# Attention values a unit later, and the split of moved blocks behind q's parts

## The chip, the cores and the metric

The kernel runs on one core of a Trainium2 chip. The time is device time in microseconds (us) for one execution. A core has five engines that work beside each other and wait for one another by semaphores: TensorE (PE in the profile; its weight loads are the row PEld), VectorE (DVE), ScalarE (ACT), GpSimd (POOL) and SyncE (SP), whose queue here issues most DMAs. Each engine takes its instructions in the order in which the program wrote them.

## The reference

One encoder block on 256 tokens of width 2048, in float32:

```
h = RMSNorm(x); [q | k | v | u] = h @ w_in
a = windowed attention: 12 query heads, 4 key/value heads of 128, |t-s| <= 128,
    ALiBi bias, a sink logit per head, softmax
f = Fourier mix of u in 4 groups of 128 channels
x = x + concat(RMSNorm(a), RMSNorm(f)) @ w_out
x = x + down(GELU(conv3(h2 @ w_gate)) * (h2 @ w_value)),  h2 = RMSNorm(x)
y = RMSNorm(x)
```

## The kernel before

Every matrix product is made with operands split in a high and a low part (`fp32r`), three products for one. So every weight tile is loaded by SP as `raw` (1 MB), copied to its high part by ScalarE (L185) and subtracted to its low part by VectorE (L186); these make `parts`. TensorE consumes one weight tile in one *unit*. The units go: 0 to 3 u, 4 to 7 v, 8 to 23 the heads of keys and queries, 24 to 39 the output projection `w_out`, then the feed-forward part.

Units 8 to 23 hold k0 q0 q1 q2, k1 q3 q4 q5, k2 q6 q7 q8, k3 q9 q10 q11. A query head whose product is in unit s passes through these steps in later units; the number is the distance from s:

- 1: its two product halves are summed (`qk_out`: ScalarE copies one half, L637; VectorE adds, L639) and made into parts (`qk_parts`: tile `qT`, ScalarE L234, VectorE L235).
- 2: TensorE multiplies by the keys (`scores`, L665, six products); VectorE adds the bias and takes the maximum (`scores_out`, L681, L685, L686); ScalarE exponentiates (`exps`, L695).
- 3: VectorE scales by the sums (`weigh`, L704, L705, L708; tile `sc`) and transposes in blocks of 32 (`turn`, L715; tile `tb`); SP writes the blocks to DRAM (tile `turn`, L720).
- 4: SP fetches the blocks back in moved order, in four DMAs (`fetch`, L726; tile `td`).
- 5: the moved blocks are split in parts (`turn_out`; tile `pt`, ScalarE L739, VectorE L740).
- 6: TensorE multiplies by the values (`values`, L768, six products into `ps_o`); ScalarE squares the result (L492) and makes its scaled high part (L234, tile `cat`), VectorE the low part (L235); GpSimd adds the square to a running sum (L497, not for head 0).

The last head, 11, skips the way through DRAM: TensorE transposes it at distance 4 (`turn_last`, L750), and its values are at 5.

The order on each engine is the program's order. In unit i the program writes: the lists `before` (values, the last head's transposes, scores), then the unit's own products, then `beside`, then the split of the weights of unit i + 2 with the load of the weights of unit i + 5 behind it on SP (`step`, `split`), and then `behind` (the exponentials). In `beside` of a unit stand, in this order: fetch, q's sum, the split of moved blocks, the last head's split, the scaling, the block transposes with their write-out, k's sum and the parts of q or k, the scores' bias and maximum, and the feature (`values_out`). The values that TensorE uses in a unit therefore need the block split of an earlier unit, and the scores in a unit the parts of q from the unit before.

Tiles used in turn: `pt`, `td`, `qT` and the sums have two buffers, `sc` and `tb` one, the weights' `raw` and `parts` three each. The units' products and, up to unit 23, the value products rotate through four PSUM banks (`mm`); scores and the value products from unit 24 on rotate through four others (`dn`). Unit 26 is the first whose products read the features of heads 4 to 7; units 29 and 31 read those of heads 8 to 11.

Of the kernel before, what the change touches and what calls it, by code (L numbers as in the profile page):

```python
# [18 lines left out]
NH = 12  # L19
# [77 lines left out]
def block_kernel(  # L97
# [316 lines left out]
    before, beside, behind = {}, {}, {}  # L414

    def at(when, i, f, *a):
        when.setdefault(i, []).append((f, a))
# [217 lines left out]
    def qk_out(kind, h, ps):  # L635
        tmp = ph.tile([P, S], F32, tag="tmp", name=f"tmp_{kind}{h}", bufs=2)
        nc.scalar.activation(tmp, ps[:, S : 2 * S], AF.Copy)  # L637
        add = ph.tile([P, S], F32, tag="add", name=f"add_{kind}{h}", bufs=2)
        nc.vector.tensor_tensor(add, ps[:, 0:S], tmp, ALU.add)  # L639
        if kind == "k":  # L640
            nc.vector.tensor_tensor(add, add, r1b, ALU.mult)
        st["add", kind, h] = add
# [135 lines left out]
        feature_out(ps, h, vcol(V_GA + h), sq_a, h == 0)  # L778


    slot_of = {kh: N_QK + n for n, kh in enumerate(QK_ORDER)}
    for i in range(N_QK, N_OUT + 8):
        heads = {i - s: h for (kind, h), s in slot_of.items() if kind == "q"}
        new = [kh for kh, s in slot_of.items() if i - s == 1]
        if i - 9 in range(NG):
            at(before, i, fourier_channels, i - 9)
        valued = [h for d, h in heads.items() if d == (5 if h == NH - 1 else 6)]
        for h in valued:
            at(before, i, values, h, mm if i < N_OUT else dn)
        turned = {d: h for d, h in heads.items() if h < NH - 1}  # L790
        last = {d: h for d, h in heads.items() if h == NH - 1}
        if 4 in last:
            at(before, i, turn_last, last[4])
        if i == 15:
            at(before, i, total, sq_f, "f")
        if 2 in heads:
            at(before, i, scores, heads[2])
        if 4 in turned:
            at(beside, i, fetch, turned[4])

        for kind, h in new:
            if kind == "q":
                at(beside, i, lambda k=kind, h=h: qk_out(k, h, st.pop(("ps", k, h))))
        if 5 in turned:
            at(beside, i, turn_out, turned[5])
        if 4 in last:
            at(beside, i, turn_last_out, last[4])
        if 3 in heads:
            at(beside, i, weigh, heads[3])
        if 3 in turned:  # L810
            at(beside, i, turn, turned[3])
        for kind, h in new:
            if kind == "k":
                at(beside, i, lambda k=kind, h=h: qk_out(k, h, st.pop(("ps", k, h))))
            at(beside, i, qk_parts, kind, h)
        if 2 in heads:
            at(beside, i, scores_out, heads[2])
            at(behind, i, exps, heads[2])
        for h in valued:
            at(beside, i, values_out, h)  # L820
# [60 lines left out]
    for n, (c, kq) in enumerate(OUT_ORDER):  # L881
        i = N_OUT + n
# [391 lines left out]
    i = up_index[n]  # L1274
# [156 lines left out]
```

## Time and profile before

| | |
|---|---|
| Median of 3 runs | 910.96 us (910.14 to 911.5) |
| Profiled execution | 908.96 us |
| Its span, first to last instruction | 907.2 us |
| TensorE / VectorE / ScalarE / GpSimd busy | 893.2 / 753.1 / 545.9 / 54.3 us |
| Granted TensorE clock | 0.998 |
| Busy in 122 to 150 us (28.0 us): TensorE, VectorE, ScalarE, GpSimd | 26.20, 24.50, 18.43, 2.67 us |

In the trace, TensorE begins the work of unit 15 at 91.00 us, of unit 19 at 118.36, of unit 23 at 145.90 and of unit 27 at 173.52; the output projection's first product is at 156.13. VectorE's first instruction of `beside` stands at 91.14 us for unit 14, 96.24 for 15, 102.46 for 16, 110.28 for 17, 118.38 for 18, 123.50 for 19, 130.52 for 20, 137.82 for 21, 145.96 for 22, 151.07 for 23, 158.31 for 24 and 166.25 for 25. So VectorE works on a unit's list while TensorE is already in the next one.

A line of a timeline has the start in us, the duration in us, the engine, the program line, the operation, the tile written and the tiles read, their shapes and the count of merged instructions. In square brackets is the idle time of the engine before the instruction and what ended it. A line of the waits has the waiting engine, tile and line, what it waited for, the total in us, how many times, and the longest.

### The profile page before, as it was taken

The numbers are of one execution on the slowest core, as the hardware profiler recorded it, in microseconds if no ns is written. First come the engines' busy times: TensorE is split into PE (matmuls) and PEld (weight loads), VectorE is DVE, ScalarE is ACT, GpSimd is POOL, SyncE is SP. The second block draws the span as 40 slices with busy tenths as digits, with TensorE's granted clock in tenths as the row PEclk, the third lists the DMA queues.
The fourth block names the chain that finished last, engine by engine and source line by source line (L and its number), as shares of the span: only waits on it lengthen the run. The fifth ranks groups of instructions, "written<-read, shape, count | busy, mean of one in ns | idle before, by whom it ended". The sixth has DMA issues, their size and how long they took to land.

```text
span 907.2 us, 12781 instructions
## 1 busy us (share of the span) xinstructions
PE 893.2 (98%) x5020; PEld 804.0 (89%) x5020; DVE 753.1 (83%) x905; ACT 545.9 (60%) x661; POOL 54.3 (6%) x65
## 2 busy tenths in 40 slices
PE   9999999999999999999999999999999999999996
PEld 7899888888899999999999999999999999999885
DVE  7569888777678877889887998978988789998996
ACT  7757576655565656557565566566656566656544
POOL 0001010110000000000000000000000000000004
PEclk9999999999999999999999999999999999999999
DMA  9965666655559687677988779797888987779652
GB/s 360 340 233 174 211 231 197 229 189 191 203 228 290 219 260 235 197 264 215 295 238 276 243 271 278 256 295 232 279 243 244 308 272 255 243 245 286 213 197 92
DMA packets 40827, 220.62 MB, mean 243 GB/s; under 512 B 4512, under 2 KB 10528, under 8 KB 16448
## 3 DMA queue, kind: packets, MB, share of 16 engines
q1 hardware_dynamic: 36512, 190.06, 56.7%
q0 software_dynamic: 4112, 29.49, 17.3%
q8 instruction: 39, 0.64, 0.3%
q10 hardware_dynamic: 144, 0.26, 0.1%
q14 instruction: 20, 0.16, 0.0%
HBM read 214.81 MB, written 4.98 MB: 242 GB/s over the span
## 4 chain that ended last, share of the span: by engine, by line
PE 81%; DVE 8%; DMA 3%; issue 3%; ACT 3%; POOL 1%; SPq 1%; ACTq 0%; POOLq 0%; DVEq 0%
PE ps_val L395 17%; PE ps_gate L395 17%; PE ps_gate L397 8%; PE ps_val L397 8%; PE ps_P L1148 3%; PE ps_P L1150 3%; PE ps_P L1149 3%; PE ps_N L1148 2%; PE ps_N L1150 2%; PE ps_N L1149 2%; DVE parts L186 2%; PE ps_u L289 2%; DMA td<-turn 2%; PE ps_a L380 2%; PE ps_a L378 2%
## 5 line engine op out<-in xcount | busy, mean ns | idle before, releaser
L186 DVE TENSOR_TENSOR parts<-raw,parts 128x2048 fp32r<-128x2048 f32 (+1 forms) x129 | 293.1, 2272 | 43.4 <-ACT parts L185 42.7
L185 ACT ACTIVATE parts<-raw 128x2048 fp32r<-128x2048 f32 (+1 forms) x129 | 245.1, 1901 | 41.7 <-PE ps_a L380 11.9
L395 PE MATMUL ps_val<-hU,parts 128*128 128x512 f32 x688 | 227.7, 382 | 0.0
L395 PE MATMUL ps_gate<-hU,parts 128*128 128x512 f32 x688 | 227.3, 382 | 0.0
L397 PE MATMUL ps_val<-hU,parts 128*128 128x256 f32 x688 | 187.5, 273 | 0.0
L397 PE MATMUL ps_gate<-hU,parts 128*128 128x256 f32 x688 | 186.9, 273 | 0.0
L395 PEld LDWEIGHTS ps_val<-hU,parts 128*128 128x128 f32 x688 | 130.0, 189 | 18.1
L395 PEld LDWEIGHTS ps_gate<-hU,parts 128*128 128x128 f32 x688 | 130.0, 189 | 18.1
L397 PEld LDWEIGHTS ps_val<-hU,parts 128*128 128x128 f32 x688 | 132.0, 192 | 0.8
L397 PEld LDWEIGHTS ps_gate<-hU,parts 128*128 128x128 f32 x688 | 131.8, 192 | 0.9
L926 ACT ACTIVATE ft_g<-ps_gate 128x256 f32<-128x256 f32 x43 | 16.5, 384 | 112.9 <-PE ps_gate L397 110.3
L395 PE MATMUL ps_q<-hT,parts 128*128 128x512 f32 x192 | 62.2, 383 | 0.0
L926 ACT ACTIVATE ft_v<-ps_val 128x256 f32<-128x256 f32 x43 | 16.5, 383 | 73.3 <-PE ps_val L397 73.3
L1148 PE MATMUL ps_P<-parts_P,op_P 128*128 128x512 f32 x144 | 54.7, 380 | 0.0
L1149 PE MATMUL ps_P<-parts_P,op_P 128*128 128x512 f32 x144 | 54.6, 379 | 0.0
L1150 PE MATMUL ps_P<-parts_P,op_P 128*128 128x512 f32 x144 | 54.6, 379 | 0.0
L397 PE MATMUL ps_q<-hT,parts 128*128 128x256 f32 x192 | 50.4, 273 | 0.0
L1034 DVE TENSOR_TENSOR parts_N<-sumw,parts_N 128x2048 fp32r<-128x2048 f32 x18 | 41.2, 2289 | 9.9 <-ACT parts_N L1033 9.9
L1148 PE MATMUL ps_N<-parts_N,op_N 128*128 128x512 f32 x108 | 41.0, 380 | 0.0
L1149 PE MATMUL ps_N<-parts_N,op_N 128*128 128x512 f32 x108 | 40.9, 379 | 0.0
L1150 PE MATMUL ps_N<-parts_N,op_N 128*128 128x512 f32 x108 | 40.9, 379 | 0.0
L395 PEld LDWEIGHTS ps_q<-hT,parts 128*128 128x128 f32 x192 | 36.1, 189 | 4.7
(347 smaller groups left out, 1554.8 us busy)
## 6 DMA issues: line engine op xcount, KB each, us to landing
raw<-in_w_up SPq DMA_DIRECT2D x86, 1024.0 KB, 6.1
raw<-in_w_in SPq DMA_DIRECT2D x20, 1024.0 KB, 5.7
sumw<-in_w_down POOLq DMA_DIRECT2D x18, 1024.0 KB, 8.5
raw<-in_w_out SPq DMA_DIRECT2D x16, 1024.0 KB, 4.8
raw<-in_w_down_late SPq DMA_DIRECT2D x4, 1024.0 KB, 5.7
u_raw<-in_u_in SPq DMA_DIRECT2D x4, 768.0 KB, 10.5
raw<-in_w_down_last SPq DMA_DIRECT2D x4, 768.0 KB, 4.6
turn<-tb SPq DMA_DIRECT2D x11, 256.0 KB, 4.2
```

What stands on the lines that cost most here:

```text
L185: nc.scalar.activation(hi, raw, AF.Copy)
L186: nc.vector.tensor_tensor(lo, raw, f32(hi), ALU.subtract)
L289: nc.tensor.matmul(ps_u[b], block(hk(k), part, b, True), in_turn(w), start=k == 0 and n == 0, stop=k == NK - 1 and n == 2,)
L378: nc.tensor.matmul(ps, ah, wh, start=first and q == q0, stop=False)
L380: nc.tensor.matmul(ps, ah, wl, start=False, stop=last and q == q0 + len(kk) - 1)
L395: nc.tensor.matmul(ps, hi[:, s], in_turn(h), start=k == 0, stop=False)
L397: nc.tensor.matmul(ps[:, 0:S], lo[:, s], in_turn(h)[:, 0:P], start=False, stop=k == NK - 1)
L926: nc.scalar.activation(tmp, ps[:, S : 2 * S], AF.Copy)
L1034: nc.vector.tensor_tensor(lo, src, f32(hi), ALU.subtract)
L1148: nc.tensor.matmul(ps, o[:, 0, p, :], wh, start=first and p == 0, stop=False)
L1149: nc.tensor.matmul(ps, o[:, 1, p, :], wh, start=False, stop=False)
L1150: nc.tensor.matmul(ps, o[:, 0, p, :], wl, start=False, stop=end)
```

## The change

Two things are changed in the schedule of units 8 to 31. The value products of heads 0 to 8 are at distance 7 instead of 6, with the feature and the running sum that follow them in the same unit; heads 9 and 10 stay at 6 and head 11 at 5. Head 6's product so moves from unit 23 to unit 24, and from the first group of PSUM banks to the second. And in `beside`, the split of the moved blocks is written behind the parts of q or k and ahead of the scores' bias, not right behind q's sum.

```diff
+    VALUES = {NH - 3: 6, NH - 2: 6, NH - 1: 5}
     slot_of = {kh: N_QK + n for n, kh in enumerate(QK_ORDER)}
     for i in range(N_QK, N_OUT + 8):
...
-        valued = [h for d, h in heads.items() if d == (5 if h == NH - 1 else 6)]
+        valued = [h for d, h in heads.items() if d == VALUES.get(h, 7)]
...
         for kind, h in new:
             if kind == "q":
                 at(beside, i, lambda k=kind, h=h: qk_out(k, h, st.pop(("ps", k, h))))
-        if 5 in turned:
-            at(beside, i, turn_out, turned[5])
         if 4 in last:
             at(beside, i, turn_last_out, last[4])
         if 3 in heads:
             at(beside, i, weigh, heads[3])
         if 3 in turned:
             at(beside, i, turn, turned[3])
         for kind, h in new:
             if kind == "k":
                 at(beside, i, lambda k=kind, h=h: qk_out(k, h, st.pop(("ps", k, h))))
             at(beside, i, qk_parts, kind, h)
+        if 5 in turned:
+            at(beside, i, turn_out, turned[5])
         if 2 in heads:
             at(beside, i, scores_out, heads[2])
             at(behind, i, exps, heads[2])
         for h in valued:
             at(beside, i, values_out, h)
```

## The prediction

> **What bounds the kernel now.** I read the page first (busy time, the slices), then the waits of the attention stage alone, then that stage's timeline engine by engine.
>
> ```profile
> PE 893.2 (98%) x5020; PEld 804.0 (89%) x5020; DVE 753.1 (83%) x905; ACT 545.9 (60%) x661; POOL 54.3 (6%) x65
> ```
>
> TensorE carries the time, so the change can move the end only where TensorE stands still. The waits from 44 to 200 us (the waiting instruction, its releaser; us in total, times, longest) say where that is:
>
> ```profile
> ACT pt L739 <- DMA td<-turn: 17.4, 8, 3.8
> ...
> DVE pt L740 <- ACT pt L739: 8.3, 7, 2.1
> ...
> PE ps_o L768 <- DVE pt L740: 2.7, 4, 0.9
> PE ps_s L665 <- DVE qT L235: 2.3, 3, 0.9
> ```
>
> TensorE waits 5.0 us in all, for two things that VectorE makes: the split of the moved blocks (pt) and q's parts (qT). ScalarE waits 17.4 us for the blocks' DMA, and VectorE 8.3 us behind ScalarE. No VectorE wait in that view is on TensorE, so in this stage VectorE sets the pace. Its rows for units 18 to 20:
>
> ```profile
> 118.38 0.42 DVE L639 TENSOR_TENSOR add_q<-ps_q,tmp_q 128x256 f32<-128x256 f32 x1
> 118.71 0.68 DVE L740 TENSOR_TENSOR pt<-td,pt 128x512 fp32r<-128x512 f32 x1
> 119.31 0.16 DVE L704 TENSOR_TENSOR sm<-sm,ex 128x2 f32<-128x2 f32 x1
> ...
> 119.71 0.62 DVE L708 TENSOR_SCALAR sc<-sc,ex 128x256 f32<-128x256 f32 x2
> ...
> 120.99 0.38 DVE L235 SCALAR_TENSOR_TENSOR qT<-add_q,qT 128x256 fp32r<-128x256 f32 x1
> 121.30 2.28 DVE L186 TENSOR_TENSOR parts<-raw,parts 128x2048 fp32r<-128x2048 f32 x1
> 123.50 0.42 DVE L639 TENSOR_TENSOR add_q<-ps_q,tmp_q 128x256 f32<-128x256 f32 x1
> 125.47 0.69 DVE L740 TENSOR_TENSOR pt<-td,pt 128x512 fp32r<-128x512 f32 x1 [1.56 <-ACT pt L739]
> ...
> 126.47 0.40 DVE L681 CUSTOM_DVE_ANT_0 sc<-ps_s,rel 128x256 f32<-128x256 f32 x1
> ...
> 127.60 0.48 DVE L235 SCALAR_TENSOR_TENSOR cat<-ps_o,vec,cat 128x256 fp32r<-128x256 f32 x1
> 128.31 2.29 DVE L186 TENSOR_TENSOR parts<-raw,parts 128x2048 fp32r<-128x2048 f32 x1 [0.24 <-ACT parts L185]
> 130.52 0.42 DVE L639 TENSOR_TENSOR add_q<-ps_q,tmp_q 128x256 f32<-128x256 f32 x1
> ...
> 132.01 1.03 DVE L708 TENSOR_SCALAR sc<-sc,ex 128x256 f32<-128x256 f32 x2
> ...
> 137.82 0.15 DVE L704 TENSOR_TENSOR sm<-sm,ex 128x2 f32<-128x2 f32 x1
> ```
>
> VectorE spends 5.12 us on unit 18, 7.02 on unit 19 (1.56 of it waiting for blocks) and 7.30 on unit 20. TensorE's row shows the dependence: it resumes at 121.43, just after qT ends (120.99 + 0.38).
>
> ```profile
> 121.43 0.71 PE L665 MATMUL ps_s<-kT,qT 128*128 128x256 f32 x4 [0.93 <-DVE qT L235]
> ...
> 156.13 0.38 PE L378 MATMUL ps_a<-parts,cat 128*128 128x512 f32 x1
> ...
> 161.32 0.38 PE L768 MATMUL ps_o<-pt,v_hi 128*128 128x256 f32 x2
> ...
> 161.98 1.14 PE L665 MATMUL ps_s<-kT,qT 128*128 128x256 f32 x6
> 162.96 0.38 PE L378 MATMUL ps_a<-parts,cat 128*128 128x512 f32 x1
> ...
> 168.14 0.38 PE L378 MATMUL ps_a<-parts,cat 128*128 128x512 f32 x1
> ...
> 175.00 0.72 PE L750 MATMUL ps_t<-ident,sc 128*128 128x128 f32 x4
> 175.48 0.46 PE L378 MATMUL ps_a<-parts,cat 128*128 128x512 f32 x1
> ```
>
> Six value products take 0.66 us (161.32 to 161.98), an output unit's own products 5.18 (162.96 to 168.14). Unit 25 begins its products 6.83 us after unit 24, and 5.18 + 2 x 0.66 would do: 0.33 lost. Unit 27 should begin them 0.66 + 0.48 us (the transposes) after 168.14 + 5.18, at 174.46, and begins at 175.48: 1.02 lost.
>
> **The change, part by part.** It adds and removes no instruction; 9 heads' value products, feature copies and running sums move a unit on, and 11 block splits move behind q's parts. ScalarE's and SP's rows that price it:
>
> ```profile
> 118.83 0.44 ACT L234 ACTIVATE qT<-add_q 128x256 fp32r<-128x256 f32 x1 [0.56 <-DVE add_q L639]
> ...
> 124.81 0.63 ACT L739 ACTIVATE pt<-td 128x512 fp32r<-128x512 f32 x1 [3.47 <-DMA td<-turn]
> ...
> 125.73 0.37 ACT L492 ACTIVATE sq<-ps_o 128x256 f32<-128x256 f32 x1
> 126.00 0.47 ACT L234 ACTIVATE cat<-ps_o,vec 128x256 fp32r<-128x256 f32 x1
> 126.36 1.92 ACT L185 ACTIVATE parts<-raw 128x2048 fp32r<-128x2048 f32 x1
> ```
>
> *Value products a unit later.* The wait on pt goes: a block split made in VectorE's unit 18 is now read in unit 20, not 19. What is late next is qT in the same units (19 and 23), so this alone gains nothing there.
>
> *q's parts ahead of the split.* In units 14, 18, 22 qT comes earlier by the split's place, 119.31 - 118.71 = **0.60 us**, and TensorE's exit from units 15, 19, 23 with it. It is counted once, because between exits VectorE's pace decides.
>
> *ScalarE's queue in units 18 and 22.* Counted from the sum's start: q's high part begins at 0.45 (118.83 - 118.38); it and the blocks' high part take 0.92 (124.81 to 125.73), then come the moved square 0.27 and feature 0.36, and the weight split's high half 1.92: its end is 3.92. VectorE's half starts at 3.95 (the same 0.03 as 128.31 after 126.36 + 1.92) and takes 2.20: the unit lasts 6.15 instead of 5.12, **1.03 longer**. The moved feature half on VectorE (0.48) is covered by that wait. In unit 14, with no values yet, it is 3.32 + 2.20 = 5.52: 0.40 longer.
>
> *Units 19 and 23.* The sum now lets q's high part start at 0.45, the blocks' follows, 1.37; weight split 3.29; VectorE's half 3.32 to 5.52, against 7.02: **1.50 shorter**. VectorE's own row of work fits (pt from 1.5, 0.6; scores 126.47 to 127.60, 1.13). It needs the blocks landed by 6.15 + 0.85 = 7.00 after 118.38; they landed 6.43 after it. SP's fetch stands behind the weight load of unit 17 as before, so that does not move; the slack is 0.57. Units 18 and 19 together: **0.47 shorter**. Unit 15 waits less, so units 14 and 15 together gain about 0.1.
>
> ```profile
> 97.41 0.69 DVE L740 TENSOR_TENSOR pt<-td,pt 128x512 fp32r<-128x512 f32 x1 [0.75 <-ACT pt L739]
> ...
> 103.40 0.69 DVE L740 TENSOR_TENSOR pt<-td,pt 128x512 fp32r<-128x512 f32 x1 [0.52 <-ACT pt L739]
> ...
> 104.39 0.88 DVE L708 TENSOR_SCALAR sc<-sc,ex 128x256 f32<-128x256 f32 x2
> ...
> 159.38 0.69 DVE L740 TENSOR_TENSOR pt<-td,pt 128x512 fp32r<-128x512 f32 x1 [0.66 <-ACT pt L739]
> ```
>
> *Units 16, 20, 24.* The blocks now have three instructions more before VectorE wants them, so the waits 0.52 (unit 16) and 0.66 (unit 24) go. Unit 16's scaling falls from 0.88 to 0.62, since its value head is now head 0, which has no running sum on GpSimd: **0.78 shorter**.
>
> *GpSimd's running sum.* It moves with the values, and it holds VectorE up:
>
> ```profile
> 131.89 0.74 POOL L497 TENSOR_TENSOR sq_a<-sq_a,sq 128x256 f32<-128x256 f32 x1 [4.78 <-ACT sq L492]
> ...
> 165.59 1.33 POOL L497 TENSOR_TENSOR sq_a<-sq_a,sq 128x256 f32<-128x256 f32 x1 [4.73 <-ACT sq L492]
> ```
> ```profile
> 166.25 0.69 DVE L704 TENSOR_TENSOR sm<-sm,ex 128x2 f32<-128x2 f32 x1
> ```
>
> The two-column sum that takes 0.15 at 137.82 took 0.69 at 166.25 and ended with GpSimd's add, at 166.9. In units 18, 20, 22 the square would end at 0.45 + 0.92 + 0.37 = 1.74 and an add of 0.74 at 2.5; qT's low half is due at 120.99 - 118.38 - 0.60 = 2.01. Bounds: nothing, if VectorE is there first, and 0.54 (0.69 - 0.15). I take **0.49**, as the add would have begun first. In unit 20 it stands against the scaling's 1.03 becoming 0.62: nothing. In units 18 and 22 VectorE's delay is covered by the split's wait, but TensorE's exit loses 0.49.
>
> The Trainium skill, page "SBUF — State Buffer", section "SBUF: two separate sides", calls this pair of ports an exclusive lock: a VectorE instruction with two SBUF inputs waits for the whole GpSimd instruction, and the other way round. The rows' scaling (1.03 against 0.62) would allow a partial delay of 0.41 and a time 0.1 us shorter; the two-column row speaks for the rule.
>
> *Sum.* VectorE at unit 22: 0.1 + 0.78 + 0.47 + 0 = 1.35 earlier. TensorE's exit from unit 23: 1.35 + 0.60 - 0.49 = 1.46. Behind it head 6's value products are now still to do, +0.66. With another 0.47 and 0.66, VectorE is 2.5 us ahead at unit 25, so the losses 0.33 and 1.02 go. Gain: 1.46 - 0.66 + 0.33 + 1.02 = **2.15 us**. Head 7's feature, wanted by unit 26's seventh to twelfth products, moves with VectorE too and stays in time. From there TensorE runs without a gap, so the gain reaches the end. The profiled execution took 908.96, 2.0 under the median of 910.96; on the median the forecast is 908.8.
>
> **Rivals.** (a) *GpSimd's add comes second and qT first.* The add's start is only 0.25 us ahead of qT. Then units 20 and 22 each give 0.49 back: gain 3.1, 907.8. (b) *TensorE waits for nothing*: all 5.0 us go, 906.0. Against it: VectorE's round stays longer than TensorE's. (c) *ScalarE's new wait eats what the DMA wait gave*: units 19 and 23 shrink by 1.03 only, unit 16 alone stays; with small parts of the last losses the gain is about 0.7, 910.3. For it: ScalarE's chain leaves nothing to spare in units 18 and 22. (d) *Slower: the blocks land later.* The write-out is issued 0.6 us earlier, now amid the fetch of the head before. If the blocks land 2.1 us later than in the rows, units 15, 19, 23 keep their length less the feature: then +0.40, +0.55 and +0.08 (units 14, 18, 20) less 0.26 (unit 16), less 0.11 for qT, +0.66 for head 6, and +0.63 more at unit 27 from units 22 to 24: 2.0 slower, 913.0. It begins past the 0.57 slack and decides from about 2.1. Against it, the view of the blocks' tile:
>
> ```profile
> DMA to landing us min/median/max: 3.6/4.7/5.4
> ```
>
> **How the numbers follow.** Chances: forecast 0.41, (a) 0.22, (b) 0.06, (c) 0.16, (d) 0.15. No change means within 0.2% (1.8 us), about what a measurement of this kernel can tell. The forecast is near that bound: 0.32 of its 0.41 is taken as faster, 0.09 as within. Faster 0.32 + 0.28 = 0.60, same 0.25, slower 0.15. The range reaches from (b), 905.9, to half of (d), 912.0.
>
> **What would show it.** Right: no TensorE wait on pt; its waits on qT stay in units 19 and 23, about 1.5 us each; VectorE's wait on ScalarE for the weight split (L186) grows by some 0.6 in units 18 and 22; ScalarE's wait for the blocks' DMA falls below 6 us; unit 27 loses nothing. Wrong: TensorE waiting for cat in unit 26, or for qT over 2.3 us; the blocks landing past 7.0 after unit 18's sum; qT 0.4 instead of 0.9 long or not delayed would be (a).

## The result and the profile after

The changed kernel takes 906.18 us, median of 5 runs (905.88 to 906.72), against 910.7 (909.1 to 911.5) for the kernel before on the same chip: a ratio of 0.9953 with a 95% interval of 0.9939 to 0.9968, so 4.3 us less (2.9 to 5.6). The profiled execution took 905.88, which is 3.08 under the 908.96 of the profiled execution before.

The page's busy time of the changed kernel: no engine does less work than before, so the gain is time in which TensorE stood still.

```profile
PE 893.2 (99%) x5020; PEld 806.3 (89%) x5020; DVE 753.7 (83%) x905; ACT 546.4 (60%) x661; POOL 56.8 (6%) x65
```

The waits of the changed kernel from 44 to 200 us (engine, tile and line, releaser; us in total, times, longest):

```profile
ACT qT L234 <- DVE add_q L639: 17.6, 12, 2.4
...
DVE parts L186 <- ACT parts L185: 8.3, 8, 1.3
...
ACT pt L739 <- DMA td<-turn: 5.5, 4, 3.2
...
DVE pt L740 <- ACT pt L739: 1.8, 2, 1.5
PE ps_s L665 <- DVE qT L235: 1.7, 2, 1.0
```

TensorE's wait on pt (2.7 before) is not in the list any more. Its wait on qT is 1.7 us for VectorE's half, with 0.5 more for ScalarE's half (2.3 in all before). ScalarE waits 5.5 us instead of 17.4 for the blocks' DMA, and VectorE 1.8 instead of 8.3 for ScalarE's part of the split. ScalarE's idle time now stands ahead of q's high part (17.6 us, for q's sum), where no block holds it.

The timeline of the changed kernel for units 18 to 20, VectorE's rows, and in unit 18 ScalarE's and GpSimd's with them:

```profile
117.13 0.42 DVE L639 TENSOR_TENSOR add_q<-ps_q,tmp_q 128x256 f32<-128x256 f32 x1
...
118.01 0.61 ACT L739 ACTIVATE pt<-td 128x512 fp32r<-128x512 f32 x1
...
118.53 0.37 ACT L492 ACTIVATE sq<-ps_o 128x256 f32<-128x256 f32 x1
118.79 0.47 ACT L234 ACTIVATE cat<-ps_o,vec 128x256 fp32r<-128x256 f32 x1
118.97 0.73 POOL L497 TENSOR_TENSOR sq_a<-sq_a,sq 128x256 f32<-128x256 f32 x1 [5.17 <-ACT sq L492]
119.14 0.90 DVE L235 SCALAR_TENSOR_TENSOR qT<-add_q,qT 128x256 fp32r<-128x256 f32 x1
119.14 1.93 ACT L185 ACTIVATE parts<-raw 128x2048 fp32r<-128x2048 f32 x1
119.95 0.68 DVE L740 TENSOR_TENSOR pt<-td,pt 128x512 fp32r<-128x512 f32 x1
...
120.55 0.48 DVE L235 SCALAR_TENSOR_TENSOR cat<-ps_o,vec,cat 128x256 fp32r<-128x256 f32 x1
...
121.11 2.29 DVE L186 TENSOR_TENSOR parts<-raw,parts 128x2048 fp32r<-128x2048 f32 x1
...
123.31 0.42 DVE L639 TENSOR_TENSOR add_q<-ps_q,tmp_q 128x256 f32<-128x256 f32 x1
...
124.32 0.48 DVE L235 SCALAR_TENSOR_TENSOR qT<-add_q,qT 128x256 fp32r<-128x256 f32 x1 [0.58 <-ACT qT L234]
...
124.83 0.69 DVE L740 TENSOR_TENSOR pt<-td,pt 128x512 fp32r<-128x512 f32 x1
...
126.64 2.29 DVE L186 TENSOR_TENSOR parts<-raw,parts 128x2048 fp32r<-128x2048 f32 x1
...
128.84 0.42 DVE L639 TENSOR_TENSOR add_q<-ps_q,tmp_q 128x256 f32<-128x256 f32 x1
...
135.54 0.15 DVE L704 TENSOR_TENSOR sm<-sm,ex 128x2 f32<-128x2 f32 x1
```

Unit 18 lasts 123.31 - 117.13 = 6.18 us, unit 19 128.84 - 123.31 = 5.53, unit 20 135.54 - 128.84 = 6.70; before they took 5.12, 7.02 and 7.30. The weight split in unit 18 starts 0.04 us after ScalarE's half ends (119.14 + 1.93 = 121.07): in that unit ScalarE's queue, longer by the moved square and feature, sets VectorE's pace. VectorE's own list ends almost level with it, at 120.55 + 0.48 = 121.03, because q's low half took 0.90; the run without the running sum, below, separates the two. In unit 19 the blocks are there (124.17 on ScalarE), and the 1.56 us wait is gone.

TensorE's timeline of the changed kernel at the places that the prediction named (exit from unit 23, first product of unit 24, values and scores before unit 25, values and transposes before unit 27, first product of the feed-forward part):

```profile
146.51 0.71 PE L665 MATMUL ps_s<-kT,qT 128*128 128x256 f32 x4 [0.70 <-DVE qT L235]
...
153.64 0.38 PE L378 MATMUL ps_a<-parts,cat 128*128 128x512 f32 x1
...
158.82 0.38 PE L768 MATMUL ps_o<-pt,v_hi 128*128 128x256 f32 x2
...
160.16 0.38 PE L378 MATMUL ps_a<-parts,cat 128*128 128x512 f32 x1
...
171.19 0.39 PE L768 MATMUL ps_o<-pt,v_hi 128*128 128x256 f32 x2
...
172.22 0.46 PE L378 MATMUL ps_a<-parts,cat 128*128 128x512 f32 x1
...
179.00 0.38 PE L378 MATMUL ps_ff<-parts,cat 128*128 128x512 f32 x1
```

Unit 24 begins 156.13 - 153.64 = 2.49 us earlier than before. The stretch before unit 25 is 160.16 - 158.82 = 1.34, which is six value products and six scores at 0.66 each and nothing lost; the one before unit 27 is 172.22 - 171.19 = 1.03, no more than products and transposes need. The feed-forward part begins 3.08 us earlier than before, where its first product stood at 182.08, and 3.08 is the whole difference of the two profiled executions.

### The profile page after: what moved, and what is told of

Read it like the earlier page. It is cut to its first block, busy times and chain, and to the rows that moved or that the text cites. A ratio compares the mean times of both kernels' runs of the same rounds, so it can differ in the third digit from the quotient of the medians.

```text
span 904.1 us, 12781 instructions
## 1 busy us (share of the span) xinstructions
PE 893.2 (99%) x5020; PEld 806.3 (89%) x5020; DVE 753.7 (83%) x905; ACT 546.4 (60%) x661; POOL 56.8 (6%) x65
## 4 chain that ended last, share of the span: by engine, by line
PE 90%; DVE 4%; issue 2%; ACT 2%; POOL 1%; ACTq 0%; POOLq 0%; DVEq 0%
PE ps_val L395 17%; PE ps_gate L395 17%; PE ps_val L397 8%; PE ps_gate L397 8%; PE ps_P L1150 3%; PE ps_P L1151 3%; PE ps_P L1152 3%; PE ps_q L395 3%; PE ps_N L1150 2%; PE ps_N L1152 2%; PE ps_N L1151 2%; PE ps_u L289 2%; PE ps_a L378 2%; PE ps_a L379 2%; PE ps_a L380 2%
## 5 line engine op out<-in xcount | busy, mean ns | idle before, releaser
L185 ACT ACTIVATE parts<-raw 128x2048 fp32r<-128x2048 f32 (+1 forms) x129 | 245.2, 1902 | 41.7 <-PE ps_a L380 12.1
```

The lines of the kernel that those rows point to most:

```text
L185: nc.scalar.activation(hi, raw, AF.Copy)
```

## The experiments

Each kernel was run in five rounds beside the kernel before (4 to 12 runs of each); where no other base is named, the edit is made on the changed kernel. The intervals are those of the ratio to the kernel before. Kernels that ran on one chip can also be compared with one another: the values alone, the split alone, the loads and the second run of the changed kernel on one; the square, the parts, the fetch and the features on another; the last four on a third.

**The changed kernel again**, beside the next three.

> The changed kernel once more, beside the kernel before on one chip. In its first profile the clock granted to TensorE was 0.53 to 0.62 from 94 to 98 us. VectorE's pace: without that dip the waits of TensorE on qT in unit 19 return (about 1.2 us instead of 0.17) and the time is the same, since VectorE's instants do not move. Rival (the dip cost 1.66 us of the time): a profile without it is 1.5 us shorter, near 902.5.

906.44 us (905.42 to 906.58), ratio 0.9952 [0.9940, 0.9965]. This run also settles a doubt about the first profile, in which the granted TensorE clock fell for some 4 us inside unit 15. That stretch in the first profile (busy us, with instructions, of TensorE, its weight loads, VectorE, ScalarE and GpSimd; then the clock, 0.57, the DMA share and GB/s):

```profile
94.00:98.00 4.00, 4.00 (x16) 3.52 (x17) 3.25 (x4) 1.57 (x4) 0.00 (x0) 0.57 0.70 213
```

TensorE's scores in units 19 and 23 of the second profile, whose clock was steady:

```profile
120.02 0.71 PE L665 MATMUL ps_s<-kT,qT 128*128 128x256 f32 x4 [0.95 <-DVE qT L235]
...
146.95 0.71 PE L665 MATMUL ps_s<-kT,qT 128*128 128x256 f32 x4 [1.39 <-DVE qT L235]
```

With the dip TensorE was late, and then hardly waited in unit 19; at full clock it came early and waited 0.95. VectorE began unit 20 at 128.84 in both, and the profiled executions took 905.88 and 906.50. TensorE had slack there, so VectorE sets the time; the dip cost nothing that can be seen.

Such a dip is not peculiar to that execution. Six of the fourteen profiles of this case have one or two in this stage: the changed kernel's first, the values alone, the split alone, the loads, the square and the fetch. In the split alone the clock is 0.63 from 96 to 100 us, in the loads 0.57 from 148 to 152. In slices of half a microsecond the granted clock is 0.50, half of full speed, for about 3.5 us (7 in one case). Each dip starts during, or less than a microsecond after, a wait of TensorE of 0.9 to 3.6 us. Such a wait does not always bring one: the second profile here has a wait of 1.02 us at the same place, ended at 93.83, and no dip. The three kernels with k's sum first, at the end of this section, have none in their profiles.

**The values a unit later, the split left at its old place.**

```diff
+        if 5 in turned:
+            at(beside, i, turn_out, turned[5])
         if 4 in last:
             at(beside, i, turn_last_out, last[4])
...
-        if 5 in turned:
-            at(beside, i, turn_out, turned[5])
```

> The value products a unit later, the block split left in its old place. VectorE's pace (my theory): TensorE's waits on pt go in units 19 and 23, but its exits stay bound by q's parts, which end where they ended (2.99 us after the sum), so nothing is gained there; the moved square and feature lengthen units 18 and 22 by about 0.4 and shorten 19 and 23 by as much, and head 6's products stand behind the exit (+0.66). Some of the loss at unit 27 goes. Together 0.5 slower to 0.7 faster than before; TensorE's waits on qT grow to about 5 us in sum, ScalarE's wait for the blocks' DMA stays above 13. Rival (what counts is that the values are not ready): the 2.7 us of waits on pt are saved, 2.5 faster or more.

910.13 us, ratio 0.9999 [0.9991, 1.0008]: nothing. The waits, 44 to 200 us:

```profile
ACT pt L739 <- DMA td<-turn: 16.8, 8, 3.5
...
PE ps_s L665 <- DVE qT L235: 4.2, 3, 2.1
```

TensorE's wait on pt is gone and its wait on VectorE's half of qT has grown from 2.3 to 4.2 (0.6 more is for ScalarE's half). The blocks' DMA holds ScalarE as long as before.

**The split moved, the values left where they were.**

```diff
-        valued = [h for d, h in heads.items() if d == VALUES.get(h, 7)]
+        valued = [h for d, h in heads.items() if d == VALUES.get(h, 6)]
```

> The block split behind q's parts, the value products at the old distance of 6. VectorE's pace: the rounds of VectorE shorten as in the whole change (ScalarE's wait for the blocks falls below 7 us), but the values of units 15, 19 and 23 now wait for a split that ends 0.6 later than q's parts: TensorE waits about 3 us on pt in each, none on qT. Gain at unit 23's exit about 1.5 of VectorE less 0.6: 0.5 to 1.5 us faster than before, a quarter of the whole. Rival 1 (order alone carries it): 4 us faster. Rival 2 (a later split can only delay the values): 2 slower.

910.25 us, ratio 0.9997 [0.9987, 1.0008]: nothing either in the median, where 0.5 to 1.5 faster was expected. The waits:

```profile
ACT pt L739 <- DMA td<-turn: 4.5, 2, 2.9
...
PE ps_o L768 <- DVE pt L740: 2.7, 3, 1.2
...
PE ps_o L768 <- ACT pt L739: 1.7, 2, 1.4
```

Now the wait on qT is gone, and TensorE waits for pt 4.4 us: the value products want the split in the very next unit, and the split comes late in VectorE's list. So each half by itself trades one TensorE wait for the other: TensorE's waits for the two tiles are 5.0 us before, 4.8 and 4.4 with one half, and 2.2 and 3.9 in the two profiles with both. Two halves that give nothing in the median make a whole of some 4 us.

The nothing of this run needs a reserve. Its twelve times follow the mean granted clock of the execution: six runs at 0.992 or 0.993 took 911.3 us in the mean, three at 0.997 or 0.998 took 908.3. The kernel before, on the same chip, took 911.4 at 0.993 (5 runs) and 909.9 at 0.997 or more (12 runs). So where the clock stays up, the split alone seems worth 1.6 us, close to what was expected, and where it dips nothing is left; three runs do not settle it.

**The kernel before, with SP's weight loads behind the next fetch.** The loads that SP issues with the splits of weights 14 to 30 now wait for the fetch of the following unit. This asks how much of the gain is the blocks' landing alone.

```diff
         halves[i] = hi, lo
+        if 14 <= i <= 30:
+            held_loads.append(i + RAW)
+            return
         load(i + RAW)
...
             at(beside, i, fetch, turned[4])
+        at(beside, i, lambda: [load(held_loads.pop(0)) for _ in held_loads[:]])
```

> The kernel before, but SP issues each weight load of units 13 to 29 behind the next unit's fetch of moved blocks, not ahead of it; nothing else moves. So the fetch no longer stands behind a load that waits for VectorE's weight split. VectorE's pace: in units 19 and 23 the blocks land about 1.7 us earlier, VectorE's waits behind ScalarE for pt fall from 8.3 to about 4, its rounds shorten by about 1.4 and the time falls by 2 to 3.5 us. Rival (the wait for the blocks is slack, only the order of q's parts and of the values decides): within 0.5 of before, the waits fall and TensorE's waits stay at 5.0.

907.83 us, ratio 0.9974 [0.9965, 0.9983]: 2.4 us faster than before, as expected. VectorE's splits of the blocks in units 18, 19 and 20 (L744 is L740 of the other kernels):

```profile
117.74 0.68 DVE L744 TENSOR_TENSOR pt<-td,pt 128x512 fp32r<-128x512 f32 x1
122.84 0.68 DVE L744 TENSOR_TENSOR pt<-td,pt 128x512 fp32r<-128x512 f32 x1
130.96 0.69 DVE L744 TENSOR_TENSOR pt<-td,pt 128x512 fp32r<-128x512 f32 x1 [2.37 <-ACT pt L743]
```

The wait in unit 19 (1.56 before) is gone, and unit 20 has one of 2.37 instead: the blocks of a later head land late, and VectorE's total wait for this split fell only from 8.3 to 6.4 us, where about 4 was expected. Blocks in time for units 19 and 23, less the new wait, are so worth 2.4 us without the rest of the change, a little over half of the 4.4 (0.48% of 910) that the changed kernel gave on this chip.

**The square written behind the scaled feature.** ScalarE's queue in value units was meant to give qT's low half its turn before GpSimd's add.

```diff
-        nc.scalar.activation(one.rearrange("p (a e) -> p a e", a=2), ps, AF.Square)
         t = cat_pool.tile([P, 512], F32R, tag="cat", name=f"cat{slot}")
         split_scaled(hi_lo(t), ps, g)
+        nc.scalar.activation(one.rearrange("p (a e) -> p a e", a=2), ps, AF.Square)
```

> The changed kernel with ScalarE's square behind its scaled copy of the feature instead of ahead of it, so GpSimd's running sum starts about 0.4 us later. Port theory (mine): in units 18 and 22 q's low part on VectorE now starts first, takes 0.38 to 0.48 instead of 0.82 to 0.90, TensorE's waits on qT there shrink by about 0.45 each, and as VectorE's own list in these units was held by the weight split only to within 0.1, its round shortens a little too: 0.3 to 0.9 us faster than the changed kernel. Rival (the long q parts are only covered work): the same within 0.2.

923.98 us, ratio 1.0148 [1.0134, 1.0162]: 13.8 us slower than before, and 17.9 slower than the kernel of the next experiment on the same chip, which is as fast as the changed one. The expectation was wrong in sign, though q's low half did shrink to 0.38 us in unit 18, as it said. ScalarE and VectorE in its unit 18 (L494 is the square):

```profile
124.28 0.48 DVE L235 SCALAR_TENSOR_TENSOR cat<-ps_o,vec,cat 128x256 fp32r<-128x256 f32 x1
124.85 0.39 ACT L494 ACTIVATE sq<-ps_o 128x256 f32<-128x256 f32 x1 [1.72 <-DVE cat L235]
125.13 1.90 ACT L185 ACTIVATE parts<-raw 128x2048 fp32r<-128x2048 f32 x1
...
127.06 2.29 DVE L186 TENSOR_TENSOR parts<-raw,parts 128x2048 fp32r<-128x2048 f32 x1 [2.31 <-ACT parts L185]
```

The square and VectorE's half of the feature read the same PSUM tile, the only tile that both touch, and the later reader in program order waits for the earlier one. So ScalarE stands still for 1.72 us until VectorE has read, its half of the weight split comes after that, and VectorE waits 2.25 to 2.31 for it in the units with values, which become 1.7 to 2.4 us longer than in the changed kernel; over the stage VectorE's wait on L185 is 27.4 us instead of 8.3. The Trainium skill, page "PSUM — Partial Sum Buffer", section "PSUM bank collisions raise a hardware error", says that accesses of different engines to one bank must be ordered, reads against reads included; the trace agrees in that the second read waited, for 1.72 us. The loss is also the strongest evidence that ScalarE's queue up to the weight split is what VectorE's round hangs on.

**q's parts ahead of the block transposes.**

```diff
             at(beside, i, weigh, heads[3])
+        for kind, h in new:
+            if kind == "q":
+                at(beside, i, qk_parts, kind, h)
         if 3 in turned:
...
-            at(beside, i, qk_parts, kind, h)
+                at(beside, i, qk_parts, kind, h)
```

> The changed kernel with q's parts on VectorE ahead of the block transposes, not behind them. Theory (q's parts in units 14, 18 and 22 release TensorE): they end about 0.6 us earlier, and in 18 and 22 before GpSimd's sum starts, so another 0.4; TensorE's waits on qT in units 15, 19 and 23 fall from about 1.0 to 1.5 to 0.1 to 0.5 each. Counted once, 0.6 to 1.1 us faster than the changed kernel, and the round of VectorE is as long as before, so no more. The write-out of the blocks is 0.35 later, which the slack of 0.5 or more in units 19 and 23 covers. Rival (VectorE's round alone decides, TensorE catches up later anyway): same within 0.2.

906.07 us, ratio 0.9953 [0.9941, 0.9965]: the same as the changed kernel, where 0.6 to 1.1 faster was expected. VectorE's parts of q come 0.9 us earlier in unit 18 (118.23 against 119.14), but the unit is no shorter (6.15 us against 6.18), because VectorE then waits 0.45 us for ScalarE's half of the weight split. Over the stage VectorE waits 9.5 us for the weight split (8.3 in the changed kernel) and 2.5 for ScalarE's split of the blocks (1.8), 0.46 of it new in unit 20. The expectation feared a later write-out of the blocks; in unit 18 SP issues it no later (119.44 against 119.59), so why unit 20 waits is not shown.

**The fetch behind the write-out on SP.**

```diff
-        if 4 in turned:
-            at(beside, i, fetch, turned[4])
...
             at(beside, i, turn, turned[3])
+        if 4 in turned:
+            at(beside, i, fetch, turned[4])
```

> The changed kernel with SP's fetch of one head's blocks behind the write-out of the next head's, so the blocks of units 15, 18, 19, 22 and 23 land about 2 to 2.8 us later; the work of every engine is the same. Theory (landing past the slack of about 0.6 is paid by VectorE, since VectorE's list stands behind the blocks' split): VectorE waits 1 to 2 us in each of units 15, 19 and 23 again, ScalarE's wait for the blocks' DMA rises from 5 to over 10; 2 to 4.5 us slower than the changed kernel, about the time of the kernel before. Rival (with the values a unit later the blocks have a whole unit of slack): within 0.5 of the changed kernel.

908.27 us, ratio 0.9976 [0.9966, 0.9986]: half of the gain is lost, at the low end of what was expected. VectorE's split of the blocks in unit 23:

```profile
153.79 0.69 DVE L740 TENSOR_TENSOR pt<-td,pt 128x512 fp32r<-128x512 f32 x1 [1.76 <-ACT pt L739]
```

Blocks that land late bring the old wait back (4.0 us in the stage instead of 1.8; ScalarE's own wait is 6.8, below the 10 expected). Only SP's order was changed, so blocks landing in time are a condition of the gain.

**The features of units 18 and 22 behind the weight split.**

```diff
-            at(beside, i, values_out, h)
+            at(behind if i in (18, 22) else beside, i, values_out, h)
```

> The changed kernel with the features of heads 2 and 5 (units 18 and 22) behind the weight split instead of ahead of it. Theory (in these units ScalarE's queue sets the weight split, 1.03 us longer than before the change): the split starts 0.63 earlier on ScalarE, VectorE's units 18 and 22 last about 5.9 instead of 6.15, and GpSimd's sum no longer meets q's parts, so TensorE's exits gain another 0.45: 0.7 to 1.2 us faster than the changed kernel. Rival (TensorE's exits do not see ScalarE's queue): units as long as before, same within 0.2.

905.59 us, ratio 0.9947 [0.9935, 0.9960]: some 0.5 us under the kernel with q's parts ahead of the transposes, on the same chip, and with intervals that overlap it is no measured gain, where 0.7 to 1.2 was expected. The mechanism is visible on VectorE:

```profile
119.16 0.38 DVE L235 SCALAR_TENSOR_TENSOR qT<-add_q,qT 128x256 fp32r<-128x256 f32 x1
120.47 2.29 DVE L186 TENSOR_TENSOR parts<-raw,parts 128x2048 fp32r<-128x2048 f32 x1 [0.33 <-ACT parts L185]
122.68 0.48 DVE L235 SCALAR_TENSOR_TENSOR cat<-ps_o,vec,cat 128x256 fp32r<-128x256 f32 x1
```

q's low half takes 0.38 instead of 0.90, and the weight split starts 120.47 - 119.16 = 1.31 after it instead of 1.97. But the feature is then paid in unit 19, which is 5.93 us long instead of 5.53. Units 18 and 19 together are 0.25 us shorter (11.46 against 11.71); most of the price is moved, not removed.

**No running sum on GpSimd.** The edit leaves out the sum of squares of heads 1 to 11.

```diff
-        if not first:
+        if not first and slot >= NH:
             nc.gpsimd.tensor_tensor(sq, sq, one, ALU.add)
```

> The changed kernel without GpSimd's running sum of the attention squares (the sum keeps head 0's square only, so the attention's norm is wrong; nothing else is left out). Port theory: q's parts of units 18, 22 and 24 on VectorE take 0.38 to 0.48 instead of 0.82 to 1.0, the two-column sum of unit 25 0.15 instead of 0.70; TensorE's waits on qT in units 19 and 23 shrink by 0.45 each. As ScalarE's weight split holds VectorE's units 18 and 22 at 6.15 anyway, only the last of these waits counts: 0.3 to 0.9 us faster than the changed kernel. Rival (their length comes from something else, as the write-out or ScalarE beside them): they stay 0.8 or longer, the time stays.

905.23 us (904.88 to 905.32), ratio 0.9941 [0.9926, 0.9957]: about 1.0 us under the changed kernel by the ratios, beside an expected 0.3 to 0.9. The two kernels ran on different chips and their intervals overlap, so the size is not settled; the mechanism is. VectorE in unit 18:

```profile
119.15 0.38 DVE L235 SCALAR_TENSOR_TENSOR qT<-add_q,qT 128x256 fp32r<-128x256 f32 x1
...
121.11 2.29 DVE L186 TENSOR_TENSOR parts<-raw,parts 128x2048 fp32r<-128x2048 f32 x1 [0.58 <-ACT parts L185]
```

The same instruction at the same moment (119.14 in the changed kernel) takes 0.38 without GpSimd's add and 0.90 with it: the add costs it 0.52. The weight split starts at 121.11 in both, so the delay of qT hides under ScalarE's queue for VectorE, as forecast, and only TensorE's exits feel it.

**k's sum at the head of the list.** The rounds with k still have a wait of VectorE on ScalarE (kT's high part). In the changed kernel, unit 17:

```profile
109.07 0.15 DVE L704 TENSOR_TENSOR sm<-sm,ex 128x2 f32<-128x2 f32 x1
...
112.50 0.82 DVE L655 TENSOR_TENSOR kT<-add_k,kT 128x256 fp32r<-128x256 f32 x1 [0.90 <-ACT kT L654]
```

```diff
         for kind, h in new:
-            if kind == "q":
-                at(beside, i, lambda k=kind, h=h: qk_out(k, h, st.pop(("ps", k, h))))
+            at(beside, i, lambda k=kind, h=h: qk_out(k, h, st.pop(("ps", k, h))))
...
         for kind, h in new:
-            if kind == "k":
-                at(beside, i, lambda k=kind, h=h: qk_out(k, h, st.pop(("ps", k, h))))
             at(beside, i, qk_parts, kind, h)
```

> The changed kernel with k's two sums on VectorE at the head of units 13, 17 and 21, as q's sum is, so ScalarE makes k's high part while VectorE scales and transposes. Theory (VectorE's round sets the pace): its wait of 0.9 for k's high part goes, units 17 and 21 last about 7.2 instead of 8.05, TensorE's exits from units 19 and 23 come 0.9 and up to 1.7 earlier, then TensorE itself begins to bound: 0.9 to 1.8 us faster than the changed kernel. The write-out of these units is 0.85 later; the fetch behind it stands behind a weight load anyway. Rival (what bounds is only the order inside units 14, 18 and 22): same within 0.3.

903.16 us (902.95 to 903.8), ratio 0.9920 [0.9905, 0.9936]: about 3.0 us under the changed kernel, more than the 0.9 to 1.8 expected. VectorE in units 17 and 18:

```profile
107.97 0.42 DVE L639 TENSOR_TENSOR add_k<-ps_k,tmp_k 128x256 f32<-128x256 f32 x1
...
110.44 0.90 DVE L655 TENSOR_TENSOR kT<-add_k,kT 128x256 fp32r<-128x256 f32 x1
...
114.99 0.42 DVE L639 TENSOR_TENSOR add_q<-ps_q,tmp_q 128x256 f32<-128x256 f32 x1
```

The wait is gone, and unit 17 is 114.99 - 107.97 = 7.02 long instead of 117.13 - 109.07 = 8.06. VectorE's waits for kT fell from four to one, so three rounds are shorter by about 1 us each. VectorE begins unit 22 at 140.95, 2.68 us earlier than in the changed kernel, and the profiled execution is 2.72 shorter (903.16 against 905.88): TensorE followed VectorE's pace one for one, which is more than the expectation had credited.

**k's sum first and the two features behind.**

```diff
+            at(beside, i, lambda k=kind, h=h: qk_out(k, h, st.pop(("ps", k, h))))
...
-            at(beside, i, values_out, h)
+            at(behind if i in (18, 22) else beside, i, values_out, h)
```

> The last edit together with the features of heads 2 and 5 behind the weight split. Theory: the gains add as long as VectorE's round is longer than TensorE's: 1.3 to 2.3 us faster than the changed kernel; TensorE's waits on qT in units 19 and 23 together under 1.5. Rival (both only take away the same wait): no better than the better one alone.

903.27 us, ratio 0.9920 [0.9904, 0.9935]: no better than k's sum alone, where 1.3 to 2.3 under the changed kernel with the two gains added was expected. The features' place adds nothing that can be measured.

**All three.** The last kernel with q's parts also ahead of the transposes; the edit is shown against that kernel.

```diff
             at(beside, i, weigh, heads[3])
+        for kind, h in new:
+            if kind == "q":
+                at(beside, i, qk_parts, kind, h)
...
-            at(beside, i, qk_parts, kind, h)
+            if kind == "k":
+                at(beside, i, qk_parts, kind, h)
```

> The last two edits and q's parts ahead of the block transposes. Theory: with VectorE's rounds shorter, q's parts 0.6 earlier now count at every exit, and TensorE's waits in units 19 and 23 are nearly gone: 1.5 to 2.8 us faster than the changed kernel. Rival: the blocks' write-out, 0.35 later on top of 0.85, makes VectorE wait for the blocks again in units 19, 20 and 23, and it is slower than without this third edit.

902.62 us (902.24 to 903.18), ratio 0.9914 [0.9898, 0.9929], the lowest median here: 7.8 us under the kernel before by the ratio, 3.5 under the changed kernel. The 0.5 us to k's sum alone lies within the intervals. Its waits of TensorE:

```profile
PE ps_o L768 <- DVE pt L740: 0.7, 2, 0.3
...
PE ps_s L665 <- DVE qT L235: 0.2, 1, 0.2
```

Of the 5.0 us that TensorE waited here before, 0.9 are left, and it is busy 155.14 of the 156.00 us from 44 to 200 (150.73 before): in this stage TensorE itself is the bound now.

## Why the prediction was right, and where its size was off

The direction and the mechanism were right; the size was not. The gain is 4.3 us where 2.15 was forecast, and 906.18 lies only 0.3 above the lower end of the range. That end was rival (b)'s time, and (b) did not come true, so that the range held is in part luck.

*The bound.* VectorE's round sets the pace and TensorE follows. It holds: a slow clock of TensorE in unit 15 cost nothing, 1.7 to 2.4 us more in VectorE's units with values cost 17.9 in all, and 1 us less in three of its rounds gave 3.0.

*Value products alone gain nothing, qT is late next.* It holds: 0.9999, with the wait moved from pt to qT. What the prediction did not say is that the other half alone gains nothing in the median too: its 0.60 for q's parts ahead of the split, and the shorter units 19 and 23, need the later values, and without them TensorE waits 4.4 us on pt.

*Lengths of units.* Forecast 6.15 for units 18 and 22 and 5.52 for 19 and 23; measured 6.18 and 5.53 in units 18 and 19, 6.13 and 5.55 in 22 and 23. For these units ScalarE's queue, counted instruction by instruction, was a good model.

*Size, first part: VectorE's gain up to unit 22 was 1.35 in the sum and came out as 2.33* (145.96 before, 143.63 after, although the stage began 0.36 us later). Three terms were too small. Units 14 and 15 together became 0.43 us shorter (5.42 + 5.47 after, 5.10 + 6.22 before) instead of 0.1; the 0.1 had no working, and the count made for unit 19, 5.52 for each of the two, would have given 0.28. Unit 16 became 1.14 shorter instead of 0.78 (7.82 to 6.68): beside the wait of 0.52 and the scaling's 0.26, the instruction behind qT's low half started 0.59 us after it before (105.95 to 106.54, the scores' bias) and starts 0.34 after it now, 0.25 less. Unit 20 became 0.60 shorter instead of 0 (7.30 to 6.70): there rival (a) came true. In the second profile it did not; the unit's split of the blocks is

```profile
131.20 1.19 DVE L740 TENSOR_TENSOR pt<-td,pt 128x512 fp32r<-128x512 f32 x1
```

1.19 instead of 0.68 long, so that GpSimd's add took back 0.5 us. There the add began at 131.02, before the split; in the first profile both are recorded at 131.20, and the split kept its 0.68. So less than 0.2 us decides which of the two is held up, and it differs from one execution to the next. In units 18 and 22 the add came first, as the sum had it: qT took 0.90 and 0.82, against a forecast of 0.87.

*The rest of the sum.* From VectorE at unit 22 the steps give 2.33 + 0.60 - 0.49 = 2.44 at TensorE's exit from unit 23; unit 24 began 2.49 earlier. The losses of 0.33 and 1.02 before units 25 and 27 went, and the 0.66 for the values that moved behind the exit was paid, ahead of unit 26: 2.49 + 0.33 + 1.02 - 0.66 = 3.18, and 3.26 was measured at unit 27 (175.48 to 172.22). Then 0.18 was lost by the feed-forward part, which leaves 3.08. No step of the sum failed in sign.

*Size, second part: the base.* 908.8 was 910.96 less 2.15, which supposed that the changed kernel's profiled execution would lie 2.0 under its median too. It lay 0.3 under it. Of the 2.6 us between forecast and result, 1.7 are this and 0.9 the terms above. Why a usual execution of the kernel before takes 1 to 2 us more than the profiled one was not shown by any trace here, and stays open; its 29 runs on one chip spread from 909.0 to 912.6, the 5 of the changed kernel there from 905.4 to 906.6. The runs show a part of it: the profiled execution had no dip and a mean granted clock of 0.998, and of those 29 runs the five at 0.993 took 911.4 us in the mean, the twelve at 0.997 or more 909.9. That dips lengthen the others is likely, since the dip in the changed kernel's first profile made TensorE 1.75 us late at unit 16 (101.37 against 99.62 in the second), and where TensorE has no slack that is time lost. But no trace of a long execution of the kernel before was kept, and even at the higher clocks the mean stays 0.9 above 908.96.

*Signs to look for.* No wait on pt: right. Waits on qT in 19 and 23 of about 1.5: 0.95 and 1.39 in the profile with a steady clock. ScalarE's wait for blocks below 6: 5.5. Unit 27 loses nothing: right. The weight split's wait on ScalarE growing by 0.6 in units 18 and 22 was not seen, because qT's delay under GpSimd's add filled it; without the add it appears, at 0.58.

*Rivals.* (b) is too strong: TensorE still waits, 3.4 us for qT in the second profile, and it took three more edits to bring that stage to 0.9. Its 906.0 is the number nearest to the measured one all the same, and (a)'s gain of 3.1 equals the 3.08 between the two profiles; both by chance, since (a) came true in unit 20 of only one profile of the changed kernel and in unit 22 of neither, and (b) in neither. (c), that ScalarE's new wait eats the gain, and (d), that the blocks land later, fall: the blocks take 4.9 us from issue to landing (median; 4.7 before) and are there in time. The fetch experiment shows the ground of (d) all the same: with blocks that come late half of the gain is gone.

## What to carry to other kernels

Where an engine other than the busiest one sets the pace, write down for each of its rounds which instruction of another engine it waits for, and count that engine's queue from the round's first instruction; here this gave the lengths of units 18, 19, 22 and 23 to 0.03 us and that of unit 14 to 0.10. Two reorderings that each swap one wait for another can be worth nothing singly and 4 us together, as here, so do not judge such a change by its halves. And look for the same waits in rounds that the change does not touch: moving k's sum was worth about 3 us, against 4.3 for the change studied here.

## What the runs showed of the hardware that was not expected

Two engines that only read one PSUM tile were kept in program order, and one reversed pair of reads made each of the rounds with values 1.7 to 2.4 us longer and cost 17.9 us in all. GpSimd's add lengthened qT from 0.38 to 0.90 us and the blocks' split from 0.68 to 1.19, and itself took 1.28 instead of 0.73 in unit 20 of the first profile, where the split kept its 0.68; without the add qT took 0.38 and the split 0.68. The granted clock fell to half for about 3.5 us in six of fourteen profiles, each time at a wait of TensorE of 0.9 us or more; in the changed kernel, where TensorE has slack, that left no trace in the time. And the spread of the times was not a property of the chip alone: on one chip, in one set of runs, it was 3.6 us for the kernel before (29 runs) and 4.2 for the split moved alone (12 runs, 907.6 to 911.8), and 1.2 for the changed kernel (5 runs). How long ScalarE waits for blocks does not explain it, since that wait is 4.5 us in the split moved alone and 5.1 to 5.5 in the changed kernel. The granted clock goes with it in the split moved alone (911.3 us at 0.992 and 0.993, 908.3 at 0.997 and 0.998); that the dips are the cause is argued, not shown.
